# RWKV-7 fronts: the Gram masks on VectorE alone, the key factor and the bonus's rate on ScalarE

## The chip, the core and the metric

One core of a Trainium2 chip runs the whole program once. The metric is the device time of one execution in microseconds (us). The kernel before took 2466.11 us, the median of three runs.

## What is computed

A backbone of two layers over 1024 latent tokens and 256 context tokens, width 1024, all float32. Layer 0 is attention; layer 1 is a bidirectional RWKV-7 branch beside a Hyena long convolution. The change lies in the RWKV-7 branch alone:

```
k_d   = k * (1 + (a - 1) * k_a)                     # key of direction d, a = sigmoid(...)
b_d   = kk * a
s     = s * w_t - (s kk_t) b_t + v_t k_t            # per head 64x64, scanned over the tokens
y     = s r_t
bonus = sum(r * 0.5 * (k_0 + k_1) * r_k) * v        # per head, both directions' keys
```

The kernel does not step token by token. It takes 64 tokens at a time, forms the products of all pairs of tokens (a Gram matrix of the scaled keys with the scaled kk and r), masks them to their triangle, inverts the triangular part, and scans over the blocks.

## The kernel before

Layer 1 first runs its input product (`gemm3`, matmuls on the tile `g_ps` with `w_hi` and `w_lo`), and then the RWKV part. That part has 8 jobs: 4 pairs of heads (j) times 2 directions (d), and each job has 5 quarters of 256 tokens, of which quarter 0 is context and the other four are latent. So 40 steps, and each has:

- a **front** (`rw_front`): it loads the keys, rates and values, forms a cumulated decay on TensorE (`cs_ps`), its exponentials on ScalarE (`E`, `AKR`, `Dt`), the key factors on GpSimd (`kd`, lines 1514 and 1516; `af`, line 1517), the scaled keys (`BK`, half on VectorE, line 1521, half on GpSimd, line 1523) and then, on TensorE, the Gram products of two heads into two tiles `g_ps`. Columns 64 to 127 of each are masked into `la` by VectorE (line 1543). Columns 0 to 63, in latent quarters alone (32 of 40 fronts, two tiles each), are copied into `gm` by ScalarE (line 1546) and masked there by GpSimd (line 1547). Four copies on ScalarE take parts of `la` into `LO` (line 1552). `la` goes to DRAM, the keys are transposed (`bk_ps`), and a right-hand side is formed (`rh_ps`). `g_ps`, `bk_ps` and `rh_ps` share two PSUM buffers for nearly all fronts, so `bk_ps` can start once the first `g_ps` is read out, and `rh_ps` once the second is.
- an **inversion** (`rw_invert`) per job: 31 steps of two VectorE instructions (lines 1595 and 1597), each on what the one before it wrote, with 31 to 256 columns. Both operands of each lie in SBUF. Job 0 is inverted in two parts of 32 and 48 rows, the other seven in one of 80 rows: 279 steps, 558 instructions.
- a **solve**, a transition and own part, and a **scan** (`S`, line 1697), with short matmuls on TensorE and copies on ScalarE.
- in direction 1, for latent quarters (16 times), a **bonus** (`rw_bonus`): six loads, then on GpSimd a sum of the two rates (line 1721), two tensor-scalar operations (lines 1722 and 1723) and a product (line 1724), then VectorE (line 1725) and a matmul. The four tiles `io` are one bonus's own: the next bonus's loads wait for them.

From step 28 the output product (`fe_ps`) is mixed in, and it is what remains at the end. Fronts run about 12 steps ahead of the scan. The order on each engine is set by the program's scheduler, from the order in the code, priorities (the inversion's is raised most) and its own estimates; on the chip each engine then takes its instructions strictly in that order, and waits at one whose operands are not there.

The tile `kd` has one buffer; `af` has three, `E` two. The constant `oka` (1 - k_a) lies in the pool `rwf`, which is closed at step 28.

Of the kernel before, what the change touches and what calls it, by code (L numbers as in the profile page):

```python
# [10 lines left out]
F32 = mybir.dt.float32  # L11
F32R = mybir.dt.float32r
AF = mybir.ActivationFunctionType
ALU = mybir.AluOpType
# [161 lines left out]
class K:  # L176
# [1064 lines left out]
    def rw_init(self):  # L1241

        nc, tc, a = self.nc, self.tc, self.a
        self.fst = ExitStack()
        self.ep = self.fst.enter_context(tc.tile_pool(name="rwe", bufs=5, side="right", reuse_waits="tile"))
        self.fpst = ExitStack()
        fp = self.fp = self.fpst.enter_context(tc.tile_pool(name="rwf", bufs=2, side="right", reuse_waits="tile"))
        self.pst = ExitStack()
        self.rpa = self.pst.enter_context(tc.tile_pool(name="rwpa", bufs=1, side="right", space=PSUM, reuse_waits="tile"))
        self.jobs = [(j, d) for j in range(4) for d in range(2)]  # L1250
        self.seq = [[0, 1, 2, 3, 4], [0, 4, 3, 2, 1]]
        self.fr, self.nf, self.inv = {}, 0, []
        C = self.C = {}
        tri = fp.tile([128, 3, 256], F32, name="tri0", tag="kkf", bufs=2)
        nc.sync.dma_start(out=tri[:, 0:2], in_=a["k_tri"].rearrange("d p k -> p d k"))
        C["tri"] = fp.tile([128, 2, 256], F32R, name="tri", bufs=1)
        nc.vector.tensor_copy(out=C["tri"], in_=tri[:, 0:2])
        C["gm"] = fp.tile([128, 2, 128], F32, name="gm", bufs=1)
        nc.sync.dma_start(out=C["gm"], in_=a["k_gmask"].rearrange("d p k -> p d k"))
        C["LO"] = [[self.ep.tile([128, 4, 128], F32, name=f"LO0{i}", tag="LO0", bufs=5) for i in range(5)]]  # L1260
        for t in C["LO"][0]:
            nc.vector.memset(t, 0.0)
        o = self.vofs["rwkv_k_a"]
        C["oka"] = fp.tile([128, 4], F32, name="oka", bufs=1)
        nc.vector.tensor_scalar(out=C["oka"], in0=self.vec[:, o:o + 4], scalar1=-1.0, scalar2=1.0, op0=ALU.mult, op1=ALU.add)

    def rw_table(self):
# [196 lines left out]
    def rw_front(self, F, q, wp, bufs):  # L1464

        nc, C, fp = self.nc, self.C, self.fp
        j, d, Dt = F["j"], F["d"], F["Dt"]
# [10 lines left out]
        af = fp.tile([128, 256], F32, name="af", bufs=3)  # L1478
# [11 lines left out]
        ps = self.rps([128, 2, 256], "cs_ps", *tags[0])  # L1490
# [9 lines left out]
        else:  # L1500
# [3 lines left out]
                             in_=ps[:, :, off:off + 65:64], func=AF.Exp, scale=-K0)  # L1504
        if d == 1 and q == 4:
            nc.gpsimd.tensor_copy(out=Dt[:, 0:1], in_=Dt[:, 20:21])
        v3 = lambda z: z.rearrange("p (q k) -> p q k", k=128)
# [3 lines left out]
        else:  # L1511
            nc.vector.tensor_tensor(out=AK, in0=AK, in1=kv, op=ALU.mult)
        kd = fp.tile([128, 2, 128], F32, name="kd", bufs=1)
        nc.gpsimd.tensor_scalar(out=kd, in0=v3(af), scalar1=self.col("rwkv_k_a", j), scalar2=C["oka"][:, j:j + 1],
                                op0=ALU.mult, op1=ALU.add)
        nc.gpsimd.tensor_tensor(out=kd, in0=kd, in1=kf, op=ALU.mult)
        nc.gpsimd.tensor_tensor(out=v3(af), in0=v3(af), in1=kv, op=ALU.mult)

# [5 lines left out]
        gm = wp.tile([128, 2, 4, 64], F32, name="gm", bufs=bufs) if lat else None  # L1524
# [16 lines left out]
        for h in range(2):  # L1541
            ps = gp[h]
            nc.vector.tensor_tensor(out=la[:, h], in0=ps[:, :, 64:128], in1=mask[:, 64:128].unsqueeze(1).to_broadcast([128, 4, 64]),  # L1543
                                    op=ALU.mult)
            if lat:
                nc.scalar.copy(out=gm[:, h], in_=ps[:, :, 0:64])
                nc.gpsimd.tensor_tensor(out=gm[:, h], in0=gm[:, h],
                                        in1=mask[:, 0:64].unsqueeze(1).to_broadcast([128, 4, 64]), op=ALU.mult)
            for c in range(2):
                s0, t0 = (0, 32) if d == 0 else (32, 0)  # L1550
                zs, t1 = slice(64 * c + s0, 64 * c + s0 + 32), 64 * c + t0
                nc.scalar.copy(out=LO[zs, 2 * h:2 * h + 2, t1:t1 + 32], in_=la[zs, h, c::2, t0:t0 + 32])
# [6 lines left out]
        ps = self.rps([128, 4, 128], "bk_ps", *tags[2])  # L1559
# [6 lines left out]
        ps = self.rps([128, 4, 128], "rh_ps", *tags[3])  # L1566
        for i in range(2):
            nc.tensor.transpose(ps[:, i::2, 0:64], AK[:, i, :], self.ident)
        for u in range(4):
            h, i = divmod(u, 2)  # L1570
# [138 lines left out]
    def rw_bonus(self, j, q):  # L1709

        nc, C, wp = self.nc, self.C, self.wp
        rows, tok = slice(j * 128, j * 128 + 128), slice(q * 256, q * 256 + 256)
        io = []
        for n, src in (("k", self.KK[rows, q, 1, :]), ("a", self.AS[0][rows, tok]), ("b", self.AS[1][rows, tok]),
                       ("r", self.US[rows, tok]), ("v", self.US[1024 + j * 128:1152 + j * 128, tok]),
                       ("g", self.G1[rows, q * 256 - 256:q * 256])):
            t = wp.tile([128, 256], F32, name=f"io{n}", tag="iovg" if n in "vg" else "io", bufs=4)
            nc.sync.dma_start(out=t, in_=src)
            io.append(t)
        k, a0, a1, r, v, g = io  # L1720
        nc.gpsimd.tensor_tensor(out=a0, in0=a0, in1=a1, op=ALU.add)
        nc.gpsimd.tensor_scalar(out=a0, in0=a0, scalar1=0.5, scalar2=-1.0, op0=ALU.mult, op1=ALU.add)
        nc.gpsimd.tensor_scalar(out=a0, in0=a0, scalar1=self.col("rwkv_k_a", j), scalar2=1.0, op0=ALU.mult, op1=ALU.add)
        nc.gpsimd.tensor_tensor(out=a0, in0=a0, in1=k, op=ALU.mult)
        nc.vector.scalar_tensor_tensor(out=a0, in0=a0, scalar=self.col("rwkv_r_k", j), in1=r, op0=ALU.mult, op1=ALU.mult)
        ps = self.rps([128, 256], "bo_ps", "r", PB[3])
        nc.tensor.matmul(ps, C["ones2"], a0, start=True, stop=True)
        nc.vector.tensor_tensor(out=v, in0=v, in1=ps, op=ALU.mult)
        return v, g
# [442 lines left out]
```

## Time and profile before

| | us |
|---|---|
| three runs | 2466.11 (median), 2457.85, 2469.48 |
| the profiled execution, its own time | 2463.09 |
| its span on the core | 2461.3 |
| TensorE matmuls busy in the span | 2212.4 |
| VectorE busy | 1548.4 |
| ScalarE busy | 1103.4 |
| GpSimd busy | 927.3 |

Busy time is a mean over stages with different limits. The stages that matter here lie behind 1770 us, where the first fronts start; the page's 40 slices (61.5 us each) show VectorE rising there while the granted TensorE clock dips. In the rows, PE is TensorE, PEld its weight loads, DVE VectorE, ACT ScalarE, POOL GpSimd, SP the queue that issues DMAs, L1543 line 1543 of the kernel. "Idle before" is the time that the engine stood just before an instruction of a group, with what ended it.

### The profile page before, as it was taken

How to read it: one execution, taken by the hardware profiler on the slowest of the kernel's cores; microseconds unless marked ns; L12 is line 12 of the kernel's file. 1: busy time of each engine (PE TensorE's matmuls, PEld its weight loads, DVE VectorE, ACT ScalarE, POOL GpSimd, SP SyncE). 2: the span in 40 equal slices, each digit the busy share in tenths (PEclk: the TensorE clock that was granted, in tenths of full speed). 3: DMA queues.
4: the chain of work that ended last, by engine and by line, in shares of the span. 5: the costliest groups of instructions: out<-in, count | busy, mean ns of one | idle time of the engine just before them, and what ended most of it. 6: DMA issues, size and time to landing. Idle time of an engine off the chain costs nothing. (4 is left out here: it accounts for less than half of the span.)

```text
span 2461.3 us, 45979 instructions
## 1 busy us (share of the span) xinstructions
PE 2212.4 (90%) x17167; PEld 1839.0 (75%) x17167; DVE 1548.4 (63%) x3091; ACT 1103.4 (45%) x2403; POOL 927.3 (38%) x959
## 2 busy tenths in 40 slices
PE   4999999999999998689899999899968888988897
PEld 3877788677877887577788787788756777777685
DVE  6255532368768877454476877566788886767524
ACT  5354434456556555532232232255444455555224
POOL 1253335301011545511132333323564555556512
PEclk8999999999999999899999999999968899998898
DMA  8433344673222666834443464474443444444522
GB/s 283 133 124 118 125 144 146 194 234 121 85 74 70 193 196 185 241 116 168 154 146 119 147 207 145 152 237 154 146 130 86 129 126 127 114 129 134 172 84 93
DMA packets 351573, 361.79 MB, mean 147 GB/s; under 512 B 83122, under 2 KB 283199, under 8 KB 350582
## 3 DMA queue, kind: packets, MB, share of 16 engines
q1 hardware_dynamic: 342038, 330.40, 44.3%
q10 hardware_dynamic: 9168, 24.25, 3.2%
q0 software_dynamic: 144, 4.19, 0.4%
q8 instruction: 136, 2.23, 0.4%
q14 instruction: 87, 0.71, 0.1%
HBM read 260.14 MB, written 100.10 MB: 146 GB/s over the span
## 5 line engine op out<-in xcount | busy, mean ns | idle before, releaser
L160 PE MATMUL g_ps<-xl,w_hi 128*128 128x512 f32 x1056 | 269.0, 401 | 1.0 <-ACT w_hi L194 1.0
L160 PEld LDWEIGHTS g_ps<-xl,w_hi 128*128 128x128 f32 x1056 | 200.1, 192 | 44.6 <-issue 2.4
L160 PE MATMUL s_ps<-k,q 128*128 128x256 f32 (+1 forms) x704 | 199.1, 379 | 7.3 <-DVE pn L702 4.0
L443 POOL TENSOR_TENSOR al_acc<-al_acc,al_t 128x512 f32<-128x512 f32 x98 | 128.8, 1314 | 186.5 <-ACT al_t L441 135.9
L198 DVE TENSOR_TENSOR w_lo<-w_raw,w_hi 128x256 fp32r<-128x256 f32 (+1 forms) x184 | 126.8, 745 | 85.3 <-PE g_ps L160 44.2
L189 ACT COPY pt<-pt_ps 128x512 f32<-128x512 f32 (+1 forms) x203 | 101.7, 505 | 137.6 <-PE pt_ps L163 131.7
L1595 DVE TENSOR_TENSOR tmp<-L,X 80x112 f32<-80x112 f32 (+28 forms) x279 | 136.9, 491 | 25.4 <-DMA L<-LD 17.0
L1597 DVE TENSOR_TENSOR X<-X,tmp 80x112 f32<-80x112 f32 (+28 forms) x279 | 136.1, 488 | 6.6
L160 PE MATMUL g_ps<-xl,w_lo 128*128 128x512 f32 x528 | 137.4, 394 | 0.0
L163 PE MATMUL pt_ps<-ident,p 128*128 128x128 f32 x704 | 119.2, 285 | 17.0 <-DVE pt L187 7.1
L160 PE MATMUL g_ps<-xhi,w_hi 128*128 128x512 f32 (+1 forms) x528 | 118.3, 366 | 8.9 <-DVE ac_res L285 4.7
L163 PEld LDWEIGHTS pt_ps<-ident,p 128*128 128x128 f32 x704 | 81.6, 143 | 52.5 <-DVE pt L187 14.2
L160 PEld LDWEIGHTS s_ps<-k,q 128*128 128x128 f32 x704 | 108.9, 198 | 14.5 <-DVE p L702 7.3
L697 ACT ACTIVATE p<-p,mn 128x1280 f32<-128x1280 f32 (+1 forms) x96 | 103.4, 1078 | 35.7 <-DVE p L702 35.6
L160 PE MATMUL g_ps<-xhi,w_lo 128*128 128x512 f32 (+1 forms) x528 | 119.0, 364 | 0.0
L883 POOL TENSOR_TENSOR bias<-namask,tt 128x384 f32<-128x384 f32 x64 | 67.7, 1059 | 129.9 <-DVE mn L892 54.1
L441 ACT ACTIVATE al_t<-al_w,condT 128x512 f32<-128x512 f32 x98 | 70.8, 722 | 98.9 <-POOL al_acc L443 62.3
L160 PEld LDWEIGHTS g_ps<-xl,w_lo 128*128 128x128 f32 x528 | 98.9, 189 | 20.9 <-issue 0.7
L160 PE MATMUL g_ps<-xlo,w_hi 128*128 128x512 f32 (+1 forms) x528 | 113.0, 356 | 0.0
L160 PEld LDWEIGHTS g_ps<-xhi,w_hi 128*128 128x128 f32 x528 | 89.9, 193 | 29.6 <-DVE qraw L551 5.4
L160 PEld LDWEIGHTS g_ps<-xhi,w_lo 128*128 128x128 f32 x528 | 89.8, 191 | 18.9 <-issue 5.8
L160 PEld LDWEIGHTS g_ps<-xlo,w_hi 128*128 128x128 f32 x528 | 89.6, 191 | 15.8 <-issue 1.9
(432 smaller groups left out, 5708.4 us busy)
## 6 DMA issues: line engine op xcount, KB each, us to landing
w_raw<-rec_w_in SPq DMA_DIRECT2D x33, 512.0 KB
hfw<-FW SPq DMA_DIRECT2D x32, 512.0 KB
w_raw<-attn_w_in SPq DMA_DIRECT2D x13, 1024.0 KB
al_w<-rec_ada_w SPq DMA_DIRECT2D x48, 256.0 KB
tt<-TG SPq DMA_DIRECT2D x64, 192.0 KB
kkf<-KK SPq DMA_DIRECT2D x40, 256.0 KB
q<-qb SPq DMA_DIRECT2D x64, 128.0 KB
HS<-hs SPq DMA_DIRECT2D x32, 256.0 KB
```

The costliest lines, as they stand in the source:

```text
L160: return self.keep(self.pe.matmul(*args, **kw))
L163: return self.keep(self.pe.transpose(*args, **kw))
L189: self.nc.scalar.copy(out=out, in_=in_)
L198: e.tensor_tensor(out=lo, in0=full, in1=hi.bitcast(F32), op=ALU.subtract)
L441: nc.scalar.activation(out=o, in_=wt, func=AF.Copy, scale=self.condT[:, k, ci:ci + 1])
L443: nc.gpsimd.tensor_tensor(out=t, in0=t, in1=o, op=ALU.add)
L697: self.nc.scalar.activation(out=p, in_=p, func=AF.Exp, bias=mn, scale=-1.0, accum_out=rs)
L883: nc.gpsimd.tensor_tensor(out=b, in0=mask, in1=tt, op=ALU.subtract)
L1595: nc.vector.tensor_tensor(out=tv, in0=L[:, s:s + 1, rt].to_broadcast([n, nj, nt]), in1=X[:, rj, s:s + 1].to_broadcast([n, nj, nt]), op=ALU ...
L1597: nc.vector.tensor_tensor(out=X[:, rj, rt], in0=X[:, rj, rt], in1=tv, op=ALU.subtract)
```

## The change

Three edits and what they need:

1. `gm` is masked by VectorE straight from PSUM (one instruction) in place of the copy on ScalarE and the product on GpSimd.
2. The key factor `af * k_a + (1 - k_a)`, the first operation on `kd`, is one activation on ScalarE in place of a tensor-scalar on GpSimd. The product with the key stays on GpSimd.
3. The bonus's factor `(a0 + a1) * 0.5 * k_a + (1 - k_a)` is one activation on ScalarE in place of two tensor-scalars on GpSimd. The sum before it and the product after it stay on GpSimd. For this there is a constant `hka` (half of k_a), and both constants lie in the pool `rwe`, which lives to the end.

```diff
-        C["oka"] = fp.tile([128, 4], F32, name="oka", bufs=1)
+        C["oka"] = self.ep.tile([128, 4], F32, name="oka", bufs=1)
+        C["hka"] = self.ep.tile([128, 4], F32, name="hka", bufs=1)
+        nc.vector.tensor_scalar(out=C["hka"], in0=self.vec[:, o:o + 4], scalar1=0.5, scalar2=None, op0=ALU.mult)
...
-        nc.gpsimd.tensor_scalar(out=kd, in0=v3(af), scalar1=self.col("rwkv_k_a", j), scalar2=C["oka"][:, j:j + 1],
-                                op0=ALU.mult, op1=ALU.add)
+        nc.scalar.activation(out=kd, in_=v3(af), func=AF.Identity, scale=self.col("rwkv_k_a", j), bias=C["oka"][:, j:j + 1])
         nc.gpsimd.tensor_tensor(out=kd, in0=kd, in1=kf, op=ALU.mult)
...
             if lat:
-                nc.scalar.copy(out=gm[:, h], in_=ps[:, :, 0:64])
-                nc.gpsimd.tensor_tensor(out=gm[:, h], in0=gm[:, h],
+                nc.vector.tensor_tensor(out=gm[:, h], in0=ps[:, :, 0:64],
                                         in1=mask[:, 0:64].unsqueeze(1).to_broadcast([128, 4, 64]), op=ALU.mult)
...
         nc.gpsimd.tensor_tensor(out=a0, in0=a0, in1=a1, op=ALU.add)
-        nc.gpsimd.tensor_scalar(out=a0, in0=a0, scalar1=0.5, scalar2=-1.0, op0=ALU.mult, op1=ALU.add)
-        nc.gpsimd.tensor_scalar(out=a0, in0=a0, scalar1=self.col("rwkv_k_a", j), scalar2=1.0, op0=ALU.mult, op1=ALU.add)
+        nc.scalar.activation(out=a0, in_=a0, func=AF.Identity, scale=C["hka"][:, j:j + 1], bias=C["oka"][:, j:j + 1])
```

How the order moves. On TensorE it is the same, matmul by matmul, up to the first front, and behind it nearly so: the same 40 steps, none moved by more than about a front, and the same rows from the 35th scan on. VectorE has 65 instructions more (64 masks, one constant), GpSimd 136 fewer, ScalarE 8 fewer (64 copies out, 56 activations in).

VectorE at the 22nd front (the first latent one of job 4), before. `la` and `gm` are the two masked parts (the `gm` after the arrow's comma is the mask constant), `tmp` and `X` the inversion's.

```order
L1597 TENSOR_TENSOR X<-X,tmp 80x17x15
L1595 TENSOR_TENSOR tmp<-L,X 80x252
L1543 TENSOR_TENSOR la<-g_ps,gm 128x256 x2
L1597 TENSOR_TENSOR X<-X,tmp 80x18x14
L1751 TENSOR_TENSOR Y<-Y,gvr 128x256
L1629 TENSOR_TENSOR R<-R,z_ps 128x512
L1595 TENSOR_TENSOR tmp<-L,X 80x247
```

The same place on VectorE now:

```order
L1750 TENSOR_TENSOR Y<-Y,gvr 128x256
L1597 TENSOR_TENSOR X<-X,tmp 80x15x17
L1544 TENSOR_TENSOR la<-g_ps,gm 128x256
L1547 TENSOR_TENSOR gm<-g_ps,gm 128x256
L1595 TENSOR_TENSOR tmp<-L,X 80x256
L1544 TENSOR_TENSOR la<-g_ps,gm 128x256
L1547 TENSOR_TENSOR gm<-g_ps,gm 128x256
L1597 TENSOR_TENSOR X<-X,tmp 80x16x16
```

The two masks of one head stand together (in 55 of 64 cases with nothing between), and between the heads stands an instruction of the inversion or none.

ScalarE at the same front, before. `S` is the scan, `LO` the copies of parts of `la`, `BT` the transposed keys.

```order
L1697 ACTIVATE S<-sy_ps,Dt 128x64
L1546 COPY gm<-g_ps 128x256
L1552 COPY LO_16901<-la 32x2x32 x2
L1546 COPY gm<-g_ps 128x256
L1552 COPY LO_16901<-la 32x2x32 x2
L1697 ACTIVATE S<-sy_ps,Dt 128x64 x2
L1563 COPY BT<-bk_ps 128x512
```

The same place on ScalarE now:

```order
L1516 ACTIVATE kd<-af,oka,vec 128x256
L1744 ACTIVATE grs<-gvr 128x4
L1697 ACTIVATE S<-sy_ps,Dt 128x64
L1745 ACTIVATE grs<-grs 128x4
L1697 ACTIVATE S<-sy_ps,Dt 128x64
L1552 COPY LO_16901<-la 32x2x32 x2
L1632 COPY At<-w_ps 128x256
L1636 ACTIVATE UV<-w_ps 64x2x128 x2
L1552 COPY LO_16901<-la 32x2x32 x2
```

The copies of `gm` are gone, those of `LO` stay and still need `la`; the `kd` shown is that of the front after this one.

The first bonus on GpSimd, before (`ioa` is the sum of the rates and what is made of it, `iok` the key):

```order
L1721 TENSOR_TENSOR ioa<-ioa,iob 128x256
L1516 TENSOR_TENSOR kd<-kd,kkf 128x256
L1517 TENSOR_TENSOR af<-af,kkf 128x256
L1722 TENSOR_SCALAR ioa<-ioa 128x256
L1523 TENSOR_TENSOR BK<-kd,E 128x2x128
L1547 TENSOR_TENSOR gm<-gm 128x256
L1723 TENSOR_SCALAR ioa<-ioa,vec 128x256
```

The factor of the fifth bonus on ScalarE now, behind a solve's copies and ahead of a front's `R`, a readout and a scan:

```order
L1632 COPY At<-w_ps 128x256
L1636 ACTIVATE UV<-w_ps 64x2x128 x2
L1722 ACTIVATE ioa<-ioa,oka,hka 128x256
L1575 COPY R<-rh_ps 128x512
L194 CAST m_19931<-yo 128x256
L1738 ACTIVATE gsq<-Y 128x256
L1697 ACTIVATE S<-sy_ps,Dt 128x64
```

So a wait for the sum of the rates, which stood in GpSimd's queue, now stands in ScalarE's, in front of copies that TensorE reads. Three bonuses also move ahead, the first from a place on VectorE behind both halves of job 0's inversion to one inside them.

## Rows read from the trace of the kernel before

**Rows 1.** Busy time by stretch: start:end, length, PE, PEld, DVE, ACT, POOL, clock

```profile
1700.00:1780.00 80.00, 78.67 (x364) 63.30 (x363) 57.48 (x59) 35.26 (x71) 40.92 (x42) 1.00 0.43 136
1780.00:1882.00 102.00, 70.87 (x562) 57.49 (x562) 89.37 (x177) 44.97 (x135) 62.67 (x79) 0.68 0.40 107
1882.00:2310.00 428.00, 371.19 (x4955) 306.61 (x4954) 323.75 (x716) 219.06 (x667) 253.81 (x358) 0.91 0.47 130
2310.00:2461.00 151.00, 135.77 (x1194) 106.16 (x1193) 53.58 (x120) 48.62 (x138) 36.66 (x53) 0.94 0.32 101
```

**Rows 2.** Shares by line of the chain that ended last, 1790 to 2310 us

```profile
by line: DVE tmp L1595 11.5%; DVE X L1597 10.8%; issue 8.6%; PE sy_ps L160 5.1%; DMA L<-LD 3.2%; PE g_ps L160 2.8%; PE y_ps L160 2.8%; PE w_ps L160 2.5%; DVE la L1543 2.4%; SPq L1606 2.1%; PE rh_ps L160 1.9%; PE z_ps L160 1.8%; DMA LD<-la 1
```

**Rows 3.** Groups by line: count, busy us, mean ns, idle before and its releaser

```profile
L1547 POOL TENSOR_TENSOR gm<-gm 128x256 f32<-128x256 f32 x64 | 49.6, 781 | 31.7 <-ACT gm L1546 28.2 <-PE sy_ps L160 3.2
...
L1514 POOL TENSOR_SCALAR kd<-af,vec,oka 128x256 f32<-128x256 f32 x40 | 38.1, 952 | 5.3 <-DMA XT<-XD 3.8
...
L1543 DVE TENSOR_TENSOR la<-g_ps,gm 128x256 f32<-128x256 f32 x80 | 31.2, 413 | 7.2 <-PE g_ps L160 6.9
...
L1546 ACT COPY gm<-g_ps 128x256 f32<-128x256 f32 x64 | 23.6, 370 | 76.4 <-DVE la L1543 75.9
...
L1521 DVE TENSOR_TENSOR BK<-af,E 128x256 f32<-128x256 f32 x40 | 21.2, 531 | 17.5 <-ACT E L1495 16.6 <-POOL af L1517 0.6
...
L194 ACT CAST sgs<-sg 128x256 fp32r<-128x256 f32 x40 | 16.6, 418 | 4.3 <-DMA sg<-SG 4.1
...
L1723 POOL TENSOR_SCALAR ioa<-ioa,vec 128x256 f32<-128x256 f32 x16 | 8.4, 523 | 1.0
L1759 ACT ACTIVATE yo<-yt_ps,vec 128x256 f32<-128x256 f32 x14 | 7.9, 566 | 4.4 <-PE yt_ps L160 4.3
L1722 POOL TENSOR_SCALAR ioa<-ioa 128x256 f32<-128x256 f32 x16 | 7.0, 436 | 0.9
```

**Rows 4.** The inversion's two lines, from the page's costliest groups

```profile
L1595 DVE TENSOR_TENSOR tmp<-L,X 80x112 f32<-80x112 f32 (+28 forms) x279 | 136.9, 491 | 25.4 <-DMA L<-LD 17.0
L1597 DVE TENSOR_TENSOR X<-X,tmp 80x112 f32<-80x112 f32 (+28 forms) x279 | 136.1, 488 | 6.6
```

**Rows 5.** One line's instructions: count, duration ns minimum/median/maximum, first and last start

```profile
L1595 DVE TENSOR_TENSOR tmp<-L,X x279: 187/403/1494, 1796.1 to 2304.0; 80x31 f32<-80x31 f32 x8, 80x87 f32<-80x87 f32 x8, 80x135 f32<-80x135 f32 x8, 80x175 f32<-80x175 f32 x8
...
L1543 DVE TENSOR_TENSOR la<-g_ps,gm x80: 402/411/425, 1781.3 to 2244.9; 128x256 f32<-128x256 f32 x80
```

**Rows 6.** Timeline, VectorE and GpSimd in job 0's inversion: start, duration, instruction

```profile
1858.71 0.90 POOL L1517 TENSOR_TENSOR af<-af,kkf 128x256 f32<-128x256 f32 x1
1859.05 0.84 DVE L1595 TENSOR_TENSOR tmp<-L,X 48x256 f32<-48x256 f32 x1
...
1859.93 0.42 DVE L1597 TENSOR_TENSOR X<-X,tmp 48x256 f32<-48x256 f32 x1
```

**Rows 7.** TensorE's waits by releaser, 1790 to 2400 us: total us, times, longest

```profile
PE bk_ps L163 <- ACT gm L1546: 18.1, 14, 2.6
...
PE g_ps L160 <- ACT gm L1546: 4.9, 2, 4.7
...
PE cs_ps L160 <- ACT gm L1546: 2.7, 1, 2.7
...
PE rh_ps L163 <- ACT gm L1546: 1.2, 5, 0.3
```

**Rows 8.** Timeline at the 22nd front's Gram read-out: start, duration, instruction, idle before

```profile
2012.62 0.74 DVE L1543 TENSOR_TENSOR la<-g_ps,gm 128x256 f32<-128x256 f32 x2
2013.07 0.37 ACT L1546 COPY gm<-g_ps 128x256 f32<-128x256 f32 x1 [2.33 <-DVE la L1543]
...
2013.49 0.66 PE L163 MATMUL bk_ps<-ident,BK 128*128 128x128 f32 x4 [1.43 <-ACT gm L1546]
```

**Rows 9.** GpSimd's wait for the bonus's rates, 1790 to 2400 us

```profile
POOL ioa L1721 <- DMA iob<-AS: 35.9, 9, 9.1
```

## The prediction

> **What bounds the kernel now.** I read the busy times by stretch first [rows 1], then the chain that ended last [rows 2], then the groups of the changed lines [rows 3]. Up to 1780 us TensorE is full (78.67 of 80 us, clock 1.00), and the change does not touch that part: its matmuls stand in the same order. From 1780 to 1882 us VectorE sets the pace: 89.37 of 102 us busy, while TensorE is busy for 70.87 us at a mean clock of 0.68. This is job 0's inversion, one long chain of dependent VectorE steps, with the first fronts between them. From 1882 to 2310 us nobody is full (TensorE 371 of 428 us, VectorE 324, GpSimd 254, ScalarE 219); time goes where one in-order queue waits for another. After 2310 us TensorE is bound again by the output product, which the change leaves alone. So all that can be won or lost lies in some 520 us, 1790 to 2310. In them the inversion's two lines hold 11.5 and 10.8% of the chain and `la`, which is the like of the new instruction, 2.4% [rows 2].
>
> **The change part by part.** The sum is made against the profiled execution, 2463.09 us (span 2461.3, so 1.8 us lie around it), which is 3.0 us under the median of 2466.11; I carry the difference over to the median.
>
> *The price on VectorE.* 64 masks are added. The nearest row is `la`: same shape, same PSUM tile, same mask constant, 413 ns of one and 80 of them in 31.2 us [rows 3]; two in a row take 0.74 us [rows 8], 0.37 each. The new order puts them in rows of two to four, so 64 x 0.37 = 23.7 us of busy time. What of it reaches the end? `la` holds 2.4% of 520 us, 12.5 of its 31.2 us, 0.40 [rows 2, 3]. The masks stand next to it, so 0.40 x 23.7 = **+9.5 us**. Ends: 0 if they only fill idle time, and 64 x 0.413 = 26.4 if all count.
>
> *What GpSimd gives up, and what that does to VectorE.* GpSimd loses 49.6 + 38.1 + 8.4 + 7.0 = 103.1 us [rows 3] of its 316.5 us in the two middle stretches [rows 1], a share of 0.33. GpSimd itself is on few places of the path; but its work slows VectorE. The inversion's step with 256 columns took 0.84 us while GpSimd ran `af`, and the step after it 0.42 us alone [rows 6]. One line's steps go from 187 to 1494 ns, while `la`, as often beside GpSimd, stays within 402 to 425 [rows 5]. So an instruction with both operands in SBUF pays, one with its data in PSUM does not. The Trainium skill (SBUF — State Buffer, "Who interferes with whom") says the same: a VectorE instruction with two SBUF inputs contends with a GpSimd instruction that reads SBUF, and whichever issues second is blocked until the first is done; one with at most one SBUF input does not contend. The trace agrees on all three counts; by the rule the masks from PSUM are safe and the sum is the one below; without it nothing is relieved, and the sum is that of the second rival.
> How much: an undisturbed step goes from 0.187 us at 31 columns [rows 5] to 0.42 at 256 [rows 6]. Steps have k x (32 - k) columns for k from 1 to 31, 176 on the mean, so 0.187 + 145/225 x 0.233 = 0.337 us. 558 of them would take 188 us; they took 136.9 + 136.1 = 273.0 [rows 4]. The excess, 85 us, is what GpSimd costs them; a third of GpSimd's work goes, so 0.33 x 85 = 28 us of it should. On the chain stand 22.3% of 520 us, 116 us of the 273, 0.425 [rows 2, 4]: **-11.9 us**. Ends: 0 if GpSimd's other work slides into the freed places, -28 if all counts.
>
> *The read-out of the Gram tiles.* TensorE waits for the copies of `gm` for 18.1 + 4.9 + 2.7 + 1.2 = 26.9 us in 22 waits [rows 7]. This looks like the prize, but it isn't: ScalarE's copy itself waited for `la`, 75.9 us in all [rows 3], and `la` for VectorE's queue. At the 22nd front `bk_ps` starts 0.87 us after the first `la` [rows 8]; with `la` and `gm` back to back on VectorE it can start 0.74 us after, and 0.05 us for the hand-over as now (ScalarE's copy ends at 2013.44, `bk_ps` starts at 2013.49): 0.79. So 22 x 0.08 = **-1.8 us**. The wait stays and changes its name. Ends: +3, if an inversion step stands between the two masks (9 of 64 places) or between the heads, and -27 if the stall went wholly.
>
> *The key factor.* 40 operations of 952 ns leave GpSimd's front chain; ScalarE takes them at 0.42 (its cast of the same shape, 418) to 0.57 (`yo`, with scale and bias, 566) [rows 3]. The front is 0.4 us shorter on that leg, but VectorE's `BK` waited for GpSimd's `af` for only 0.6 us in all, against 16.6 for ScalarE's `E` [rows 3]. I take **-1 us**, ends -4 and +4: `kd` has one buffer, so ScalarE must now wait until GpSimd has read the front before.
>
> *ScalarE.* It gives 64 x 0.370 = 23.6 us and takes 56 x 0.418 = 23.4 (31.7 at 566). In the two stretches it is 264 of 530 us busy: covered, nothing. *The bonus.* Two operations of 436 and 523 ns become one of 0.42 and two hand-overs; VectorE's line waits behind them as before. Nothing, unless ScalarE is held up (rival below).
>
> Sum: 9.5 - 11.9 - 1.8 - 1 = -5.2 us. 2463.09 - 5 = 2458 for the profiled kind of execution, **2461 us** on the median's scale.
>
> **The rivals.** *The freed port wins more.* VectorE sets the pace from 1780 to 1882 us, where GpSimd is busy for 62.67 of 102 us [rows 1]. If the inversion's whole relief counts, since every step there is on the chain and the later fronts start sooner, it is -28 for -11.9: -21 in all, 2445. For it: the chain of rows 2; against it: in the long stretch no engine is full.
>
> *VectorE pays in full.* If GpSimd's other reads slide into the places, nothing is relieved: 9.5 - 1.8 - 1 = +7, 2473; and if the masks fall where VectorE is full, all 26.4 count: +24, 2490. It decides from about 15 us of masks on the path on. The Trainium skill (Perfetto Trace Analysis, "Optimizing Scalar/DVE Operations") speaks for this one: if VectorE is saturated, work may better go to ScalarE, the reverse of edit 1. The trace shows VectorE saturated for one fifth of the 520 us alone.
>
> *ScalarE stands at the bonus.* GpSimd waited 35.9 us, nine times, for the rates' loads [rows 9], and nobody minded. The factor now stands in ScalarE's queue, behind that sum, with `R`, `BT` and the scan's `S` behind it, for which TensorE waits. If half of the wait is passed on, +18 - 5 = +13, 2479; all of it, +31, 2497. It decides once ScalarE comes to the factor before the sum is done. Against it: in the order the factor mostly stands behind copies of a later step (the fifth bonus's behind a whole solve), so that the sum has time. For it: the first bonuses moved ahead, to a place where loads have less lead.
>
> *It doesn't do what it says.* The order shows all three edits in place; I give this nothing.
>
> **How the numbers follow.** The forecast, relief and price about equal: 0.47, its own range 2453 to 2473. The port wins more: 0.32, about 2445, 2435 to 2453. VectorE pays in full: 0.10, 2473 to 2490. ScalarE stands: 0.11, 2479 to 2497. A measurement of this kernel can tell about 0.5% from no change, 12.3 us, so faster is under 2453.8 and slower above 2478.4. Faster 0.32, from the port's case. Same 0.47 from the forecast and 0.04 from VectorE's lower end: 0.51. Slower 0.06 + 0.11 = 0.17. The range reaches down to 2439, which leaves out 0.08 of the port's case, and up to 2482, which leaves out 0.11 of the slower ones.
>
> **What would show it.** Right: `gm` on VectorE 64 times at about 0.37 to 0.41 us; the inversion's lines at a mean near 440 ns for 491 and 488 (273 - 28 = 245 us for 558); GpSimd's busy time down by about 100 us and ScalarE's unchanged; TensorE's waits for `gm` now on VectorE, still over 20 us. The stretch of job 0's inversion should shrink by a few us. Wrong: inversion steps as slow as before (no relief); TensorE's waits for `gm` gone (then the read-out was worth more than I gave it); ScalarE idle before line 1722 for over 10 us, and TensorE behind it. What could prove it wrong altogether is the order: a few steps shift on every queue, and waits that depend on loads landing may move either way by several us.

## The result, and the profile after

| | us |
|---|---|
| changed kernel, seven runs | 2449.63 (median), 2441.05 to 2457.04 |
| kernel before, on the same chip | 2466.11 (median), 2457.85 to 2475.42 |
| ratio | 0.9928, interval 0.9906 to 0.9950 |
| profiled execution after, its own time and span | 2450.84, 2449.1 |

The change gains 0.72% (0.50 to 0.94), some 18 us by the ratio; forecast were 5. The time lies inside the range, nearer to the rival "the freed port wins more" (2445) than to the forecast (2461). By the bound of 0.5% this is faster, to which 0.32 was given.

The stretches after, cut as in [rows 1]. The columns are length, busy time of TensorE, its weight loads, VectorE, ScalarE, GpSimd, then the granted clock and the DMA's share and rate:

```profile
1780.00:1882.00 102.00, 72.40 (x629) 58.83 (x627) 88.15 (x204) 47.66 (x135) 44.45 (x54) 0.66 0.48 132
1882.00:2310.00 428.00, 375.37 (x4950) 309.10 (x4950) 322.03 (x752) 223.49 (x654) 193.14 (x253) 0.93 0.48 129
```

GpSimd is down by 18 us in the first and by 61 in the second. VectorE, which has 64 instructions more, is as busy as before: what it gained and what it was given cancel. The groups by line say so one by one (count, busy us, mean ns, idle before); they answer to [rows 3, 4]:

```profile
L1597 DVE TENSOR_TENSOR X<-X,tmp 80x112 f32<-80x112 f32 (+28 forms) x279 | 129.8, 465 | 6.3
L1595 DVE TENSOR_TENSOR tmp<-L,X 80x112 f32<-80x112 f32 (+28 forms) x279 | 122.5, 439 | 32.7 <-DMA L<-LD 24.8 <-POOL X L1590 1.6
L1544 DVE TENSOR_TENSOR la<-g_ps,gm 128x256 f32<-128x256 f32 x80 | 32.7, 413 | 10.8 <-PE g_ps L160 10.6
L1547 DVE TENSOR_TENSOR gm<-g_ps,gm 128x256 f32<-128x256 f32 x64 | 26.3, 410 | 0.0
L1516 ACT ACTIVATE kd<-af,oka,vec 128x256 f32<-128x256 f32 x40 | 24.0, 600 | 16.5 <-POOL BK L1524 13.8 <-DMA af<-AS 2.3
L1722 ACT ACTIVATE ioa<-ioa,oka,hka 128x256 f32<-128x256 f32 x16 | 9.6, 599 | 19.5 <-POOL ioa L1721 19.4
```

The inversion's two lines took 252.3 us for 273.0, a mean of 452 ns; the masks' records add to 26.3, but they overlap their neighbours' (the point on the masks, further down). The waits for the second masked part, by TensorE, and for GpSimd, by ScalarE (total us, times, longest), answer to [rows 7]:

```profile
PE bk_ps L163 <- DVE gm L1547: 10.7, 13, 2.3
PE rh_ps L163 <- DVE gm L1547: 5.7, 1, 5.7
PE cs_ps L160 <- DVE gm L1547: 3.1, 1, 3.1
PE g_ps L160 <- DVE gm L1547: 2.3, 1, 2.3
...
ACT ioa L1722 <- POOL ioa L1721: 19.4, 10, 7.0
...
ACT kd L1516 <- POOL BK L1524: 13.3, 21, 2.3
```

TensorE's four rows add to 21.8 us, for 26.9 before: most of the stall stays and has a new name. ScalarE now stands for 33 us at what the change gave it.

### The profile page after: what moved, and what is told of

The parts are those of the page before. It is cut to its first block, busy times and chain, and to the rows that moved or that the text cites. A ratio compares the mean times of both kernels' runs of the same rounds, so it can differ in the third digit from the quotient of the medians.

```text
span 2449.1 us, 45918 instructions
## 1 busy us (share of the span) xinstructions
PE 2198.6 (90%) x17167; PEld 1826.2 (75%) x17167; DVE 1543.8 (63%) x3156; ACT 1111.4 (45%) x2395; POOL 842.2 (34%) x823
## 5 line engine op out<-in xcount | busy, mean ns | idle before, releaser
L1595 DVE TENSOR_TENSOR tmp<-L,X 80x112 f32<-80x112 f32 (+28 forms) x279 | 122.5, 439 | 32.7 <-DMA L<-LD 24.8
L1597 DVE TENSOR_TENSOR X<-X,tmp 80x112 f32<-80x112 f32 (+28 forms) x279 | 129.8, 465 | 6.3
L160 PEld LDWEIGHTS g_ps<-xl,w_lo 128*128 128x128 f32 x528 | 98.5, 188 | 20.7 <-issue 0.5
```

The lines of the kernel that those rows point to most:

```text
L160: return self.keep(self.pe.matmul(*args, **kw))
L1595: nc.vector.tensor_tensor(out=tv, in0=L[:, s:s + 1, rt].to_broadcast([n, nj, nt]), in1=X[:, rj, s:s + 1].to_broadcast([n, nj, nt]), op=ALU ...
L1597: nc.vector.tensor_tensor(out=X[:, rj, rt], in0=X[:, rj, rt], in1=tv, op=ALU.subtract)
```

## The experiments

All edits are made in the changed kernel or in the one before, with the fronts, jobs and loads as they are (one run alone reorders a bonus's loads). Where a run's stage is spoken of, it is the time from the first `cs_ps` weight load to the end of the span. Ahead of it, up to the first front's own loads, TensorE's, ScalarE's and GpSimd's queues of the two kernels are the same, instruction by instruction, and yet that start lay between 1767.1 and 1778.6 us in single profiles: a whole span carries a scatter that the stage does not. The stage of the changed kernel was profiled twice, 680.7 and 679.7 us; no other kernel's was.

### One edit at a time, and two

The edits are those of the diff above: the first alone, the second alone, the third alone, and the first two.

> The mask of gm on VectorE alone; the key factor and the bonus's factor stay on GpSimd. Theory (a freed read port pays most of the price on VectorE): GpSimd loses 49.6 us, VectorE gains 26, the inversion's mean falls from 490 to about 465 ns; 2 to 10 us faster than before, so most of the change's 16 us is this edit's or needs all three. Rival (the read-out of the Gram tiles is what pays): the whole 16 us here. Rival (VectorE pays in full): not faster, and the gain is the other edits'.

> The key factor on ScalarE alone. Theory: GpSimd loses 38 us, ScalarE gains 40 x 0.60 = 24 us, VectorE nothing; the inversion's mean falls by some 10 to 20 ns; 2 to 6 us faster. Rival (order and waits at the one buffer of kd): no gain or up to 5 us slower, with ScalarE idle before line 1515 for over 10 us.

> The bonus's factor on ScalarE alone. Theory: within 3 us of before; GpSimd loses 15 us, ScalarE gains 16 x 0.60 = 10 us. Rival (ScalarE stands at the bonus): ScalarE idle for some 20 us before the factor and 5 to 15 us slower.

> The change without the bonus's edit. Theory: as the change, 10 to 18 us faster than before, since the bonus's edit is worth nothing. Rival (ScalarE stands at the bonus, 19.4 us idle in the changed kernel): 5 us or more faster than the change, about 2443 us.

| run | ratio, interval | inversion, busy us |
|---|---|---|
| first edit | 0.9982, 0.9965 to 0.9999 | 258.2 |
| second edit | 0.9985, 0.9969 to 1.0002 | 272.2 |
| third edit | 1.0008, 0.9992 to 1.0023 | 274.8 |
| first and second | 0.9998, 0.9984 to 1.0013 | 253.8 |
| all three | 0.9928, 0.9906 to 0.9950 | 252.3 |

The times of the three single edits lie where their theories had them. But the second was to lower the inversion's mean by 10 to 20 ns, and left it at 488 ns for 489; and the two edits together met neither their theory (10 to 18 us faster) nor the rival (2443 us).

Two readings. The inversion is relieved by the first edit; its lines there are

```profile
L1596 DVE TENSOR_TENSOR X<-X,tmp 80x112 f32<-80x112 f32 (+25 forms) x279 | 130.1, 466 | 6.5
L1594 DVE TENSOR_TENSOR tmp<-L,X 80x112 f32<-80x112 f32 (+25 forms) x279 | 128.1, 459 | 26.9 <-DMA L<-LD 15.1 <-POOL X L1589 5.5
```

and with the second edit alone, though GpSimd loses the 38.1 us of its factor, they are nearly as slow as before:

```profile
L1596 DVE TENSOR_TENSOR X<-X,tmp 80x112 f32<-80x112 f32 (+27 forms) x279 | 138.7, 497 | 7.1
L1594 DVE TENSOR_TENSOR tmp<-L,X 80x112 f32<-80x112 f32 (+27 forms) x279 | 133.5, 479 | 27.9 <-DMA L<-LD 16.4 <-POOL X L1589 5.2
```

And the times don't add: the three single ones, each known to about 0.17%, give 0.25% together, the whole 0.72%, and two edits nothing, with the inversion as short as in the whole. So something beside the work of each edit moves the time. Two theories were put up for the rest: **W**, that it is work (the bonus on GpSimd costs the 14 us that lie between the medians of two edits and of three), and **O**, that it is the order, which the scheduler draws anew on every queue after any edit.

### The same work in other orders

The bonus's factor as one operation on GpSimd; two lines of the front swapped, with all three edits and with two; and the rates loaded ahead of the key:

```diff
-        nc.scalar.activation(out=a0, in_=a0, func=AF.Identity, scale=C["hka"][:, j:j + 1], bias=C["oka"][:, j:j + 1])
+        nc.gpsimd.tensor_scalar(out=a0, in0=a0, scalar1=C["hka"][:, j:j + 1], scalar2=C["oka"][:, j:j + 1], op0=ALU.mult, op1=ALU.add)
```

> The changed kernel with the bonus's factor on GpSimd, as one operation with the constants hka and oka, not on ScalarE. GpSimd loses half of what it loses by the third edit (16 of 32 operations, about 8 us of busy time). Theory W (the work: once the Gram parts and the key factor are moved, GpSimd's operations at the bonus cost the 12 us that stand between the two edits alone, 2463.6, and all three, 2449.6): half of the operations, so about half of the 14 us, 2455 to 2459. Theory O (the order: each edit redraws the order on all queues, and by that the stage wins or loses 5 to 10 us whatever the work): anywhere from 2447 to 2466, with no rule; what the time does then shows in TensorE's clock and waits between the 5th and the 20th scan, not at the bonus. By both the inversion's steps stay at the relieved 440 to 465 ns, since the Gram part is off GpSimd.

```diff
-        nc.gpsimd.tensor_tensor(out=kd, in0=kd, in1=kf, op=ALU.mult)
         nc.gpsimd.tensor_tensor(out=v3(af), in0=v3(af), in1=kv, op=ALU.mult)
+        nc.gpsimd.tensor_tensor(out=kd, in0=kd, in1=kf, op=ALU.mult)
```

> The changed kernel with two lines of the front in the other order: GpSimd's product for af ahead of its product for kd. The work on every engine is the same to the instruction; only the order drawn from it differs. Theory W: as the changed kernel, within 3 us, 2447 to 2453, or a little faster, as af no longer stands behind ScalarE's factor. Theory O: off by 5 us or more is as likely as not, 2443 to 2462.

> The first two edits without the third, with the same two lines in the other order. Theory W: as the two edits before, 2461 to 2466. Theory O: may fall as low as all three edits do, 2448 to 2466; a time under 2458 speaks for O, as GpSimd's bonus is there in full.

```diff
-        for n, src in (("k", self.KK[rows, q, 1, :]), ("a", self.AS[0][rows, tok]), ("b", self.AS[1][rows, tok]),
+        for n, src in (("a", self.AS[0][rows, tok]), ("b", self.AS[1][rows, tok]), ("k", self.KK[rows, q, 1, :]),
```

> The changed kernel with the bonus's two rates loaded ahead of its key, so that the sum on GpSimd waits less. GpSimd waited 51.6 us in 12 waits for the second rate. If the bonus's chain stands on the path (theory W), this gives 2 to 6 us more, 2444 to 2448, and ScalarE's 19.4 us ahead of the factor shrink. If those waits cost nothing and the order decides (theory O), the waits shrink by a third or so and the time lies anywhere within 2445 to 2460.

| run | us, median | ratio, interval |
|---|---|---|
| bonus's factor as one GpSimd operation | 2459.93 | 0.9984, 0.9967 to 1.0000 |
| all three, two lines swapped | 2455.07 | 0.9965, 0.9944 to 0.9985 |
| two edits, two lines swapped | 2464.78 | 0.9987, 0.9969 to 1.0005 |
| all three, rates loaded first | 2463.68 | 0.9988, 0.9973 to 1.0003 |

The last one speaks against W most plainly, though it lies above the range that O was given as well (2445 to 2460). GpSimd's wait for the second rate fell from the first of these rows (changed kernel) to the second (rates first), and the kernel with it was 0.6% slower than the changed one:

```profile
POOL ioa L1721 <- DMA iob<-AS: 51.6, 12, 9.0
```

```profile
POOL ioa L1721 <- DMA iob<-AS: 37.4, 11, 7.4
```

The swap of two lines, which changes no work at all, leaves half of the gain. At 2455.07 us it is outside W's range and inside O's. The other two don't decide: 2459.93 is just over W's figure and within O's, 2464.78 within both.

### The order held still

For these the old program is built first and its order read off; every instruction that both kernels have is then chained to the one ahead of it on its engine, so that the queues stay as they were, and only what an edit adds finds its own place.

```diff
+        last = {}
+        for k in order or []:
+            if k in at:
+                if k[0] in last:
+                    tc.add_manual_dep(at[k], last[k[0]].name,
+                                      mybir.DependencyInfo(mybir.DependencyClass.NoSync, mybir.DependencyReason.DATA), reason="order")
+                last[k[0]] = at[k]
```

> The changed kernel once more, beside the three below. By both theories within its first interval, a ratio of 0.9906 to 0.9950, or 2443 to 2455 us. Nearer to 0.9965 than to 0.9928 would say that the first seven runs flattered it and that the orders differ by less than they seem.

> All three edits, but every instruction that both kernels have is held to the place in its engine's queue that it had before the change: TensorE's order is that of before matmul by matmul, and the new instructions (64 masks, 56 activations, one constant) are set between the old ones. Theory W (the work): as all three edits, 2445 to 2453. Theory O (the work gives the sum of the prediction, about 5 us, and the rest came with the new order): 2457 to 2464. If the work gives nothing or costs (the masks outweigh the relief): 2466 to 2472.

> The reverse: no edit at all, but every instruction that both kernels have stands where the changed kernel's order has it. Theory W: as before, 2463 to 2469. Theory O: the order's own part, about 12 us of the 16.5, 2451 to 2458, and with the edits' 5 us it makes up the changed kernel's time.

In the last one the edit is

```diff
-                    nc.gpsimd.tensor_tensor(out=gm[:, h], in0=gm[:, h], in1=gk, op=ALU.mult)
+                    nc.gpsimd.memset(gm[:, h], 0.0)
```

> The kernel before in its own order on every queue; only GpSimd's 64 products on gm are 64 memsets of the same tile, which read nothing (the masked part is zero by this, so that part of the computation is left out). It measures the read port alone, with no mask on VectorE. If GpSimd's reads slow the inversion: its two lines fall from a mean of 491 and 488 ns to about 455 to 465, 15 to 20 us of busy time as in the first edit alone, and with the prediction's share of 0.425 on the path the time falls by 6 to 9 us, 2457 to 2460; by all of it, if the whole relief counts, 2446 to 2451. If it is GpSimd's time and not its reads that counts, or other reads slide in: the inversion stays over 480 ns and the time at 2463 to 2468.

| run | us, median | ratio, interval | stage, us | inversion, busy us |
|---|---|---|---|---|
| before (its first profile) | 2465.00 | 1 | 690.1 | 273.0 |
| all three, their own order, again | 2446.87 | 0.9934, 0.9912 to 0.9957 | 679.7 | 254.0 |
| all three, old order | 2457.18 | 0.9972, 0.9954 to 0.9990 | 682.7 | 252.2 |
| old work, new order | 2466.41 | 1.0007, 0.9991 to 1.0022 | 696.3 | 270.7 |
| product without reads, old order | 2450.52 | 0.9949, 0.9928 to 0.9969 | 676.1 | 258.7 |

So the gain is real: it came again. With the order held, the work of the three edits is worth 7 us (2 to 11); W, which wanted 2445 to 2453, falls. But O as it was put falls too: the new order gives the old work nothing, where it should have given 12 us. What is left is both together. By these medians the order drawn for the new work suits that work and not the old: in it the edits are worth 0.73%, in the old one 0.28%; the difference between the two orders with the same new work is 9 us (2 to 17, from the two ratios and their intervals). The single profiles' stages show only 2 to 3 of them, so how much of the 9 belongs to the order of the stage, and the place in the queues where it arises, stay open. That the order counts by several us the stages do show: the same new work has 679.7 and 680.7 us in its own order, 682.7 in the old one, 684.5 with the two lines swapped and 688.3 with the rates first; two edits alone have 696.9, and 690.3 with the lines swapped.

Where the work gains can be read from the end of job 0's inversion, counted from the first `cs_ps`. It came after 110.6 us before, 104.3 in both profiles of the changed kernel, 102.4 with all three edits in the old order and 103.6 without the product's reads. In the old order these 8.2 us are the whole gain of the stage (7.4): behind job 0 the relief and the price of the masks cancel. Without the masks the 7 us at job 0 grow to 14.0 by the end.

The last row of the table shows the product's reads without the masks. Here nothing was added to VectorE, and no queue was changed; GpSimd's product became a memset of the same tile, so the masked part is left out of the result. The groups of that kernel, busy us and mean ns:

```profile
L1606 DVE TENSOR_TENSOR X<-X,tmp 80x112 f32<-80x112 f32 (+28 forms) x279 | 130.0, 466 | 6.6
L1604 DVE TENSOR_TENSOR tmp<-L,X 80x112 f32<-80x112 f32 (+28 forms) x279 | 128.7, 461 | 23.8 <-DMA L<-LD 15.8 <-POOL X L1599 1.3
...
L1557 POOL MEMSET gm<- 128x256 f32 x64 | 19.4, 311 | 35.5 <-ACT gm L1556 31.9 <-PE sy_ps L160 3.2
```

One place shows it by itself. This is the timeline of the kernel before, an inversion step with 207 columns that starts just after the product (start, duration, instruction):

```profile
2155.93 0.72 POOL L1547 TENSOR_TENSOR gm<-gm 128x256 f32<-128x256 f32 x1
2155.95 0.94 DVE L1595 TENSOR_TENSOR tmp<-L,X 80x207 f32<-80x207 f32 x1
```

and this is the same step, starting just after the memset:

```profile
2146.73 0.31 POOL L1557 MEMSET gm<- 128x256 f32 x1
...
2146.77 0.37 DVE L1604 TENSOR_TENSOR tmp<-L,X 80x207 f32<-80x207 f32 x1
```

0.94 us against 0.37, which is what a step of this width takes with no operation of GpSimd beside it. The Trainium skill (SBUF — State Buffer, "Who interferes with whom") says that such a VectorE instruction contends with a GpSimd instruction that reads SBUF, not with one that only writes it; both rows agree.

The whole stage, from the first `cs_ps` on, in the columns of [rows 1]: before, the changed kernel, all three in the old order, and the product without reads.

```profile
1771.00:2461.00 690.00, 585.50 (x6758) 476.57 (x6756) 471.08 (x1021) 317.97 (x954) 359.55 (x497) 0.89 0.43 121
```

```profile
1768.00:2449.00 681.00, 579.48 (x6757) 471.46 (x6755) 469.49 (x1085) 326.11 (x945) 276.02 (x361) 0.90 0.44 123
```

```profile
1774.00:2457.00 683.00, 578.05 (x6758) 470.94 (x6757) 467.98 (x1085) 326.77 (x945) 269.70 (x362) 0.89 0.44 122
```

```profile
1772.00:2448.00 676.00, 575.33 (x6756) 468.92 (x6754) 453.14 (x1021) 316.94 (x954) 328.85 (x496) 0.90 0.44 124
```

VectorE, the third busy time of each row, drops by 18 us where only the relief is had (14.3 of them the inversion's), and by 2 to 3 where the masks come with it.

## Why the prediction was right, and where it was not

The direction, the range and the mechanism held; the forecast itself was 11.4 us too high, and two of the sizes behind it were wrong. Point by point:

- **What the forecast's sum describes** is the work of the edits, and with the order held still that work measured -7 us (-11 to -2) against -5.2. What it had no term for is the order. It was named at the end as something that may move "either way by several us"; by the medians it moved 9 us (2 to 17) to the good side, by the stages 2 to 3. Other orders of the same work lie 2 us to the good (the swapped lines, 0.9965) and 4 to the bad (the rates first, 0.9988) of the old order's 0.9972, so this was one draw of several, and a lucky one.
- **The share of the relief on the path is the step that failed.** 0.425 of it was to count, from the inversion's part of the chain. The product without reads took 14.3 us from the inversion and 12.6 (8 to 18) from the kernel: 0.88 (0.5 to 1.2), and still 0.70 of the 17.9 us that VectorE as a whole lost. That each step waits for the one before, so that a shorter step moves all that follow, would explain it; no run shows this reason by itself. The part that the lines hold of the chain does not tell the share. After the change it is as large as before, 22.2% for 22.3, and in the second profile of the same kernel 18.7%:

```profile
by line: DVE X L1597 11.1%; DVE tmp L1595 11.1%; issue 8.2%; DMA L<-LD 3.9%; PE sy_ps L160 3.8%; PE w_ps L160 3.7%; PE y_ps L160 3.5%; PE fe_ps L160 2.7%; DVE AKR L1512 2.2%; DMA LD<-la 2.1%; PE ph_ps L160 2.1%; PE g_ps L160 2.0%; PE bk_ps 
by line: DVE tmp L1595 9.4%; issue 9.4%; DVE X L1597 9.3%; PE sy_ps L160 5.0%; PE y_ps L160 3.9%; PE g_ps L160 3.1%; DMA L<-LD 3.1%; SPq L1606 2.6%; DMA UV<-VT 2.6%; PE w_ps L160 2.5%; PE z_ps L160 2.3%; SPq L1558 2.2%; PE ph_ps L160 2.1%; 
```

  A reserve: the memset is also 30 us shorter on GpSimd than the product (49.6 to 19.4), and no run took that time away and left the reads. Some of the 12.6 may be GpSimd's own. It can't be much of what others wait for directly: other engines waited 5.5 us for the product in the trace of before, 4.9 of them one TensorE weight load, and 4.4 for the memset. The second edit alone took the 38.1 us of the factor off GpSimd (20.7 net, as its other operations got longer), with the inversion as it was, and gained 0.15% (-0.02 to 0.31), in an order of its own.
- **The size of the relief** was forecast as 28 us, by GpSimd's lost share of a third; it was 20.7. The third was taken over all that GpSimd gives up, but 53.5 of the 103.1 us were operations with one input tensor, which cost the inversion little. The trace of before has the price of each, over the inversion steps that began while an operation of GpSimd ran, with at least 150 ns of it to go. A step's loss is counted here over the median of its width with no operation beside it (272 such steps; 196 ns at 31 columns, 421 at 256).
  - Beside the `gm` product 574 ns of it were left on the mean and the step lost 452 (34 steps, 15.4 us in all). In 33 of them the loss was what was left, less 134 to 148 ns.
  - Beside the `kd` factor 632 were left and the step lost 138 on the mean (29 steps, 4.0 us). That mean mixes two cases: 18 steps lost 160 to 259 ns, and 11 lost nothing, while the factor itself took 0.79 to 2.10 us instead of 0.55 at its shortest.
  - The bonus's two tensor-scalars cost 1.9 us (15 steps).
  - In the run with the memset, 202 were left and the step lost nothing (13 steps).

  The three prices add to 21.3 us, a quarter of the excess of 85, where 20.7 were measured; the product alone stood at 15.4, where taking its reads away gave 14.3. The smaller prices are not confirmed one by one: the second edit alone relieved 0.8 us and the third -1.8, and two profiles of the same kernel differ by 1.7.
- **The price and the rest** (masks, read-out, key factor: +9.5, -1.8, -1) were given +6.7. If all of the 20.8 us of relief in the old order count at 0.88, that is -18.3, and with -7 in all the rest comes to some +11. It is an estimate from two intervals, each 4 to 5 us to either side, so +6.7 is not ruled out. On these figures the relief's term and the rest were both too small, with opposite signs: that -5.2 lies so near to -7 is luck in part.
- **The masks** have records of 410 ns each, but VectorE's records overlap by about 80 ns when the next instruction does not need the result of the last. At the 22nd front of the changed kernel they start every 0.33 us:

```profile
2003.91 0.41 DVE L1544 TENSOR_TENSOR la<-g_ps,gm 128x256 f32<-128x256 f32 x1
2004.24 0.41 DVE L1547 TENSOR_TENSOR gm<-g_ps,gm 128x256 f32<-128x256 f32 x1
2004.57 0.41 DVE L1595 TENSOR_TENSOR tmp<-L,X 80x256 f32<-80x256 f32 x1
```

  `la` and the masks, laid over each other, keep VectorE busy for 53.1 us, where `la` alone had 31.2: 21.9 us for 64 masks. So the 0.37 of the forecast, 23.7 us, was about right, and 64 times 410 ns is too much.
- **The read-out** went nearly as said: 21.8 us of TensorE's waits stayed under a new name, where a forecast from [rows 7] alone would have hoped for 27. They are 5.1 us fewer than before, not 1.8; in the old order 16.0 are left.
- **GpSimd** lost 85.1 us of busy time on the page (927.3 to 842.2), not 100. Its other products got longer: the one on `kd`, 772 to 871 ns, and its part of `BK`, 945 to 1045. **ScalarE** went from 1103.4 to 1111.4 us, not level, as its new operations take 0.60 us and not 0.42 to 0.57.
- **The rivals.** "The freed port wins more" has its time, and it has its mechanism, but in the old order the whole change is 7 us, so its 21 are not shown. "VectorE pays in full" fell: the inversion was relieved. "ScalarE stands at the bonus" saw its sign, 19.4 us ahead of line 1722, and the matmul behind it, `bo_ps`, waited 7.1 us for VectorE, where it had waited 1.9; the price of 13 to 31 us it did not have. Whether the third edit helps by itself stays open: kernels with it stand at 0.9931 to 0.9988, with the first two alone at 0.9987 and 0.9998, alone at 1.0008.

## What to carry to other kernels

Work that one engine takes over can be paid by what it sheds elsewhere: look at which operands of its neighbours lie in the shared memory before counting instructions. What a relief is worth can be priced from the trace: pair each step with the operation that ran as it began, and add up what the steps lost; here that gave 21 us for 20.7, where the share of busy time gave 28. The serial chain of short steps returned most of its relief here (12.6 of 14.3 us), twice what its part of the chain said, and that part itself differed between two profiles of one kernel; price relief and added work apart, and not by the chain alone. And where a scheduler draws the order, an edit of a few us comes with a new draw worth as many; measure it once with the order held, and once or twice with lines swapped that change nothing, before keeping or dropping it for its own sake.

## What the runs showed that was not expected

- An activation on ScalarE with both scale and bias from SBUF took 600 ns for 128x256 (585 to 615), where a cast of the same shape took 418 and `yo`, with scale and bias but from PSUM, 566 [rows 3].
- VectorE's two-input steps that began beside GpSimd's product on `gm` ended as if they had started about 0.14 us before its end (33 of 34 steps). Beside the `kd` factor, with one input tensor, either the step waited (18 of 29) or the factor was drawn out, to as much as 2.10 us. A memset held up none of 13.
- The same kernel work in four orders spread from 0.9931 (the two measurements of the changed kernel taken together) over 0.9965 and 0.9972 to 0.9988, 14 us.
